# Attention's output projection as seven block products, and the gates' input sums made on VectorE during the attention

## The chip, the cores and the metric

One core of a Trainium2 chip runs the whole kernel as one program. The metric is the device time of one execution in microseconds, the median over several executions. TensorE (PE in the profile) does the matmuls, VectorE (DVE) and ScalarE (ACT) the elementwise work, GpSimd (POOL) a few elementwise operations and the issue of some DMAs, SyncE (SP) issues most other DMAs. Each engine takes its instructions in the order in which the program lists them and stops at the first one whose inputs, or whose place to write to, are not ready.

## The reference

A residual block on a sequence of 1024 tokens of width 1024, all in float32. Cut to what bears on the change:

```
xn = rmsnorm(x, norm1_g)
u  = xn @ w_in      # q,k,v of attention; f,i,q,g of the recurrence; gate_sb, gate_hg
o_sb = stick_breaking_attention(q_sb, k_sb, v_sb)        # 1024 x 512
o_hg = rmsnorm(hgrn2(...), hg_norm_g) * silu(g_hg)       # 1024 x 512
g_a  = sigmoid(gate_sb + b_gate[:1024])
g_b  = sigmoid(gate_hg + b_gate[1024:])
merged = g_a * (o_sb @ w_o_sb) + g_b * (o_hg @ w_o_hg)   # w_o_sb: 512 x 1024
h = x + merged @ w_out
h = h + square(relu(rmsnorm(h) @ w_ff1)) @ w_ff2
out = rmsnorm(h, final_g)
```

## The kernel before

Activations lie transposed: channels on the 128 partitions, tokens along the free dimension, in tiles of 128x1024 (two blocks of 128 channels by one half of 512 tokens, or one block by all 1024 tokens). A float32 product is made of three matmuls on operands that are split in a high part and a remainder: `three` issues high x high, high x remainder, remainder x high into one PSUM bank of 512 columns. The high part is a cast on ScalarE (`hi_copy`, rows CAST at L156), the remainder a subtraction on VectorE (`lo_sub`, rows TENSOR_TENSOR at L161). In names, a trailing `h` or `hi` is a high part, `l` or `lo` a remainder, `r` a raw tile as loaded.

The order in the program: norm and the first projections; then stick-breaking attention, in which each of the items (a head's block of queries) has scores `z`, a scan on VectorE (`rm`), a transpose on TensorE (`pw`), a split into `wTh` (ACT) and `wTl` (DVE), and the product `po`; between its pieces projection matmuls are interleaved by `st.advance`. Then the four heads of the HGRN2 recurrence, whose "main" pieces (`sl`, a score product that needs the ScalarE copy `ksl` of the keys made by `scores_of`; `pk`, `pkv`, `pho`, `pot`) alternate on TensorE with "fill" blocks. Fill blocks are `raw_job` (gate products that are kept in DRAM, `pga`, `pgq`), and then `sb_job`: attention's output projection, `pys`. After head 3 come the gates (`gates()`), with products `gX`, `gY` for ten gate blocks, and after that the merge, `w_out` and the MLP.

The parts that the change touches:

- **Attention's output projection.** `sb_job(cp)`, four units `wo00` to `wo03` of 256 output columns each. A unit's weights are one 128x1024 tile, split once (ACT and DVE). For each of its two blocks of 128 output channels and each half of the tokens, 4 channel blocks x 3 matmuls fill one bank `pys{cb}_{i}`: 4 x 2 x 2 x 12 = 192 matmuls. The first half is multiplied by the gate `g1r` (a DRAM load) on VectorE and stored by POOL, the second is copied by ScalarE (`ys`) and stored by ACT's queue. The attention output `osr` is split into `asbh`, `asbl` ahead of the projection. Three units lie among the recurrence's head 3; the last, `wo03`, lies in the gates: four steps after `y5` of the first gate block (`SB_HELD`), and the rest between `x7` and `y3`.
- **Inputs of the gates.** The gates are themselves block products with fewer multiplications (a Strassen-like scheme), so they need sums of quarters of the normed input `xn`. `whole_input` adds high part and remainder together by DMAs that accumulate (`xnl<-xnh`, eight of 512 KB on POOL's queue); then `sum_forms`, advanced a step at a time by the projection's loop, makes `gs` tiles by eight VectorE additions of 128x1024 and splits each (`gsh` on ACT, `gsl` on DVE).
- **Weight sums of `w_out`** are made by POOL's accumulating DMAs during attention, one per second item (`wsums`).

Instruction order on each engine is set by a scheduler from the order of this code and the declared dependencies (`after` adds one for order alone); tiles come from pools, and a tile's first writer waits for the last reader of the tile that had its place before. `slot` is a pool of 128x1024 tiles, `half` of 128x512, `wpool` has two tiles each of `raw`, `whi`, `wlo` kinds.

Of the kernel before, what the change touches and what calls it, by code (L numbers as in the profile page):

```python
# [2 lines left out]

# [6 lines left out]
F32 = mybir.dt.float32  # L10
F32R = mybir.dt.float32r
# [28 lines left out]
def kernel(  # L40
# [1264 lines left out]
            s = slice(half * 512, (half + 1) * 512)  # L1305
            return h[:, s], l[:, s]

    a_sb, a_hg = Split("asb"), Split("ahg")
    mgs = Acts("ms")
    def half(name, dt=F32):  # L1310
        return hpool.tile([P, 512], dt, tag="h", name=name)
# [87 lines left out]
    def raw_job(cb):  # L1399
        u = raw_units[cb]  # L1400

        def steps_of(ps, wt, w0, half_, k0, start):
            wh, wl = u.hl[wt]
            for k in range(4):
                c = (w0 + k) * P
                xh, xl = xn.mov(k0 + k, half_)
                three(
                    ps, wh[:, c : c + P], wl[:, c : c + P], xh, xl, start and k == 0, k == 3, True
                )
                if k % 2 == 1:  # L1410
                    yield

        def body():
            p1, p14, g1 = (half(f"{n}_{cb}") for n in ("p1", "p14", "g1"))
            ps, p4 = bank(f"pga{cb}"), bank(f"pgq{cb}")
            if 6 <= cb < KT:
                load_g1(cb - 6)
            if 5 <= cb < KT:
                sb_units[cb - 5].load()
            if 3 <= cb < KT - 1:  # L1420
                osb[cb - 3] = slot(f"osr{cb}")
                load(osb[cb - 3], od[cb - 3])
            yield from steps_of(ps, 0, 0, 0, 0, True)
# [7 lines left out]
            if cb == 3 or cb == KT - 1:  # L1431
                whole_input(1, int(cb == KT - 1))
# [8 lines left out]
            if 4 <= cb < KT:  # L1441
                a_sb.put(cb - 4, osb.pop(cb - 4))

        return st.add([u], body)

# [2 lines left out]
    def load_g1(cb):  # L1448
        g1r[cb] = half(f"g1r{cb}")
        load(g1r[cb], gd[cb])  # L1450

    forms, whole = {}, {}
    WAIT = 7

    def whole_input(i, j):
        for kp in range(2):
            h, l = (t.bitcast(F32) for t in xn.t[i, 2 * j + kp])
            nc.gpsimd.dma_start(l, h, accum_op=ALU.add)
            whole[i, j, kp] = l

    def sum_forms():


        raw = whole
        def split(m, kp, src):
            forms[m, kp] = tuple(slot(f"gs{n}{m}{kp}", F32R) for n in "hl")
            hi_lo(*forms[m, kp], src)

        for j in range(2):
            whole_input(0, j)  # L1470
        yield from range(WAIT)
        s1, s2 = {}, {}
        for kp in range(2):
            s1[kp] = slot(f"gs1{kp}")
            ins = add(s1[kp], raw[1, 0, kp], raw[1, 1, kp])
            if kp == 0:
                after(ins, hg_sum[0])
            yield
        for kp in range(2):
            split(5, kp, s1[kp])  # L1480
            yield
        for kp in range(2):
            s2[kp] = slot(f"gs2{kp}")
            sub(s2[kp], s1[kp], raw[0, 0, kp])
            yield
            split(6, kp, s2[kp])
            yield
        gates_in[0].load()
        gates_in[0].load_sums()
        for kp in range(2):  # L1490
            s3 = slot(f"gs3{kp}")
            sub(s3, raw[0, 0, kp], raw[1, 0, kp])
            split(7, kp, s3)
            yield
        gates_in[0].split()
        for kp in range(2):
            s4 = slot(f"gs4{kp}")
            sub(s4, raw[0, 1, kp], s2[kp])
            split(3, kp, s4)
            yield  # L1500
        gates_in[1].load()

    sb_units = []

    def sb_job(cp):
        src = W_OSB[:, cp * 256 : (cp + 1) * 256].rearrange("(k p) c -> p k c", p=P)
        unit = Unit(f"wo0{cp}", [[(0, 256, src)]])
        unit.roomy = (0,)
        sb_units.append(unit)

        def body():
            if cp == 0:
                side.append(sum_forms())
            for j in range(2):
                cb = 2 * cp + j
                if 1 < cb + 1 < KT:
                    load_g1(cb + 1)
                g1 = g1r[cb]
                for i, cs in halves():
                    ps = bank(f"pys{cb}_{i}")  # L1520
                    for _ in proj_half(
                        ps, unit.hl[0], a_sb.mov, 4, i, lambda k: k * 256 + j * P
                    ):
                        next(side[0], None)
                        yield
                    if i == 0:
                        mul(g1, ps, g1)
                        nc.gpsimd.dma_start(yd[cb][:, i, :], g1)
                    else:
                        y = half(f"ys{cb}")  # L1530
                        nc.scalar.copy(y, ps)
                        nc.scalar.dma_start(yd[cb][:, i, :], y)

        return st.add([unit], body)


    for h in range(1, NHS):
# [12 lines left out]
    f_job(3)  # L1550
    q_job(3)
    j_raw = [raw_job(cb) for cb in range(KT)]
    j_sb = [sb_job(cp) for cp in range(4)]

    class GatePair:
        def __init__(self, cb):
# [2 lines left out]
        def load(self):  # L1559
            cb = self.cb  # L1560
            self.raw = [
                wpool.tile([P, 1024], F32, tag="raw", name=f"wg{cb}r{i}") for i in range(2)
            ]
            for i, s_, which in ((0, 0, 0), (0, 1, 1), (1, 1, 1)):
                load(
# [72 lines left out]
        def gated(self, which, first, second):  # L1638
            h = 2 * (self.cb - KT) + which

            def rest(u2_sum):
                if which == 1:
                    muls(u2_sum)
                a_hg.put(h, ohg[h], u2_sum)

            def muls(behind=None):
                for (_, cs), t in zip(halves(), (first, second)):
                    after(mul(ohg[h][:, cs], ohg[h][:, cs], t), behind)

            if which == 0:  # L1650
                muls()
            owed_gated.append(rest)

        def x6(self):
# [741 lines left out]
    n_fill = 9 * (NHS - 1 + 5) + 10  # L2396
    n_first = 4
    ready = deque()
    wsums = out_weight_sums()
    done = 0  # L2400
    for i, it in enumerate(items):
        if i + 1 < len(items):
# [153 lines left out]
```

## Time and profile before

| | |
|---|---|
| median of 3 runs | 1419.76 us (1419.75 to 1419.99) |
| profiled execution, its own time | 1420.01 us |
| its span in the profile | 1418.2 us |
| granted TensorE clock, mean | 0.999 |
| TensorE, busy | 1408.0 us |
| VectorE, busy | 1049.5 us |
| ScalarE, busy | 659.3 us |
| GpSimd, busy | 145.0 us |

The span is what the trace covers; the time of the execution has 1.8 us more. Busy times are sums over instructions that overlap in part: a matmul's record is longer than the step to the next one, so TensorE's rate is read from start to start. Attention's products `po` lie between 91 and 327 us; the projection's matmuls `pys` between 511.7 and 573.6 us, with the first gate products `gX` from 554.7 us between them.

### The profile page before, as it was taken

What the parts mean: (1) busy time and instruction counts of PE and PEld (TensorE: products, weight loads), DVE (VectorE), ACT (ScalarE), POOL (GpSimd) and SP (SyncE); (2) the same over time, 40 slices, a digit from 0 to 9 for tenths busy, and PEclk for the clock granted to TensorE, in tenths of its full rate; (3) what the DMA queues carried; (4) which work ended last, traced back from release to release, by engine and by line L of the source; (5) the groups of instructions that cost most, each with busy time, mean ns of one, the idle gap of its engine ahead of it and who ended that gap; (6) DMA issues with size and microseconds to landing.
All of it is one profiled execution on the core that took longest, in us unless ns stands there. A gap on an engine that the chain in (4) does not pass through costs nothing.

```text
span 1418.2 us, 18602 instructions
## 1 busy us (share of the span) xinstructions
PE 1408.0 (99%) x6848; PEld 1183.5 (83%) x6848; DVE 1049.5 (74%) x1429; ACT 659.3 (46%) x1127; POOL 145.0 (10%) x282
## 2 busy tenths in 40 slices
PE   9999999999999999999999999999999999999998
PEld 7888888888888888888888888888888888888886
DVE  6667777778567888887788897676766657668765
ACT  6455555554243554433244764445444443534343
POOL 3011223110011031000000300000000000000042
PEclk9999999999999999999999999999999999999999
DMA  8344445435135685364585514444446974776725
GB/s 253 83 119 127 104 101 102 104 77 154 60 75 169 224 223 186 120 214 156 162 298 194 186 53 170 163 163 142 138 145 239 351 269 148 278 274 242 273 97 186
DMA packets 169730, 241.91 MB, mean 171 GB/s; under 512 B 30844, under 2 KB 97960, under 8 KB 169640
## 3 DMA queue, kind: packets, MB, share of 16 engines
q1 hardware_dynamic: 151432, 192.48, 41.0%
q0 software_dynamic: 11616, 34.61, 9.9%
q10 hardware_dynamic: 6592, 13.63, 2.7%
q8 instruction: 54, 0.88, 0.3%
q14 instruction: 36, 0.29, 0.1%
HBM read 170.43 MB, written 68.16 MB: 168 GB/s over the span
## 4 chain that ended last, share of the span: by engine, by line
PE 97%; ACT 1%; DMA 1%; DVE 1%; issue 0%; POOL 0%; SPq 0%; POOLq 0%; DVEq 0%; ACTq 0%
PE pm L128 21%; PE pX L128 9%; PE pW L128 6%; PE pY L128 6%; PE pjqk L128 6%; PE pga L128 4%; PE gX L128 4%; PE gY L128 4%; PE pjf L128 3%; PE pjq L128 3%; PE pys L128 3%; PE pji L128 3%; PE pyh L128 3%; PE po L128 3%; PE z L128 2%; PE pwX L128 2%
## 5 line engine op out<-in xcount | busy, mean ns | idle before, releaser
L854 DVE TENSOR_TENSOR_SCAN rm<-rm,bits 128x512 f32<-128x512 f32 (+6 forms) x72 | 87.5, 1222 | 30.5 <-ACT rm L835 29.0
L156 ACT CAST whid<-w 128x1024 fp32r<-128x1024 f32 x30 | 31.6, 1054 | 153.8 <-PE pm L128 85.4
L128 PE MATMUL pm<-wlod,sh 128*128 128x512 f32 x240 | 93.6, 390 | 0.0
L128 PE MATMUL pm<-whid,sl 128*128 128x512 f32 x240 | 93.5, 389 | 0.0
L128 PE MATMUL pm<-whid,sh 128*128 128x512 f32 x240 | 93.4, 389 | 0.0
L128 PE MATMUL pm<-tl,sh 128*128 128x512 f32 (+1 forms) x210 | 81.3, 387 | 0.0
L128 PE MATMUL pm<-th,sl 128*128 128x512 f32 (+1 forms) x210 | 81.3, 387 | 0.0
L128 PE MATMUL pm<-th,sh 128*128 128x512 f32 (+1 forms) x210 | 81.3, 387 | 0.0
L161 DVE TENSOR_TENSOR wlod<-w,whid 128x1024 fp32r<-128x1024 f32 x30 | 36.7, 1222 | 55.0 <-ACT whid L156 54.8
L156 ACT CAST wTh<-pw 128x512 fp32r<-128x512 f32 (+2 forms) x96 | 43.7, 482 | 62.4 <-PE pw L131 60.8
L161 DVE TENSOR_TENSOR wTl<-pw,wTh 128x512 fp32r<-128x512 f32 (+2 forms) x96 | 50.5, 548 | 28.9 <-ACT wTh L156 28.6
L161 DVE TENSOR_TENSOR sl<-sa,sh 128x1024 fp32r<-128x1024 f32 x56 | 68.2, 1218 | 0.6 <-ACT sh L156 0.6
L2173 POOL TENSOR_SCALAR fss<-fss 128x1 f32<-128x1 f32 x8 | 4.3, 543 | 562.0 <-ACT fsc L2168 561.5
L156 ACT CAST sh<-sa 128x1024 fp32r<-128x1024 f32 x56 | 57.2, 1045 | 7.8 <-DMA sa<-ad 7.8
L128 PEld LDWEIGHTS pm<-wlod,sh 128*128 128x128 f32 x240 | 45.1, 188 | 9.9 <-DVE wlod L161 0.4
L128 PEld LDWEIGHTS pm<-whid,sh 128*128 128x128 f32 x240 | 45.0, 188 | 9.4
L128 PEld LDWEIGHTS pm<-whid,sl 128*128 128x128 f32 x240 | 45.1, 188 | 9.2
L128 PE MATMUL pX<-sqh,t1l 128*128 128x512 f32 x128 | 50.0, 390 | 0.0
L128 PE MATMUL pX<-sql,t1h 128*128 128x512 f32 x128 | 50.0, 390 | 0.0
L128 PE MATMUL pX<-sqh,t1h 128*128 128x512 f32 x128 | 49.8, 389 | 0.0
L128 PEld LDWEIGHTS pm<-th,sh 128*128 128x128 f32 x210 | 39.5, 188 | 8.1
L128 PEld LDWEIGHTS pm<-tl,sh 128*128 128x128 f32 x210 | 39.4, 188 | 8.0
(936 smaller groups left out, 4358.8 us busy)
## 6 DMA issues: line engine op xcount, KB each, us to landing
w<-in_w_ff_dram SPq DMA_DIRECT2D x72, 512.0 KB, 4.8
sa<-ad SPq DMA_DIRECT2D x52, 512.0 KB, 6.8
ad<-a SPq DMA_DIRECT2D x32, 256.0 KB, 4.5
ad<-s SPq DMA_DIRECT2D x16, 512.0 KB, 3.2
tw<-in_w_out_dram POOLq DMA_DIRECT2D x24, 256.0 KB, 5.8
pr<-pd SPq DMA_DIRECT2D x10, 512.0 KB, 5.8
x<-in_x_dram SPq DMA_DIRECT2D x8, 512.0 KB, 7.9
xnl<-xnh POOLq DMA_DIRECT2D x8, 512.0 KB, 6.2
```

The lines of the kernel that those rows point to most:

```text
L128: return pe(nc.tensor.matmul(*a, **k))
L156: hi_last[0] = after(in_turn("act", nc.scalar.copy(dst, src)), hi_behind[0])
L161: nc.vector.tensor_tensor(out=dst, in0=src, in1=hi.bitcast(F32), op=ALU.subtract),
L854: sc = nc.vector.tensor_tensor_scan(out=rr, data0=rr, data1=bits[:, 1024 - nk + a : 1024 - nk + b][:, ::-1], initial=rm[:, b : b + 1] if i ...
L2173: nc.gpsimd.tensor_scalar(out=ssq, in0=ssq, scalar1=1.0 / D, scalar2=EPS, op0=ALU.mult, op1=ALU.add)
```

## The change

The projection `o_sb @ w_o_sb` becomes seven block products in place of eight. Weights and activations are taken as 2 x 2 blocks (256 input channels by 512 output channels; 256 input channels by 512 tokens). Seven products, in the order 2, 5, 3, 1, 6, 7, 4 (`SB_ORDER`), each of four banks (4 blocks of 128 output channels) x 2 channel blocks x 3 matmuls = 24 matmuls, 168 in all. Products 3, 6, 7 and 4 accumulate in PSUM on banks that stay open from an earlier product (`start` is true for 2, 5 and 1 alone), 5 and 3 share the names `pysY`, and 1, 6, 7, 4 share `pysX`. `end` takes each bank out: ScalarE copies after 2, 5, 3 and 4 (`aw`, `ay`, `az`), VectorE additions and subtractions after 1, 6 and 7, with the gate's multiplication where a sum is complete.

The weight blocks' sums (`tv1` to `tv4`) are made in DRAM by eight accumulating DMAs on POOL's queue during the attention, and are loaded as `wo{m}r`. Each of the seven weight blocks is split (`sb_split`: one CAST of 128x1024 on ACT, one subtraction on DVE), two products ahead. Activation blocks are summed on VectorE (`sb_sums`, eight operations of 128x512) and split (`sb_form`: `ash{m}`, `asl{m}`), one product ahead.

The gates' input sums are no longer made by `whole_input` and the eight additions: `input_sums` makes them from the high parts and remainders on VectorE, 18 operations of 128x1024 (`xs`, `xs4`), one per step of the attention's loop with `i > 2 and i % 5 > 1`, and POOL stores eight results to DRAM (`sx`). `sum_forms` then only loads them (`gs`) and splits them. The first gate block's raw weights move from `wpool` to `slot`; `SB_HELD` is 5 in place of 4 steps.

Cut to its core:

```diff
-    def whole_input(i, j):
-        for kp in range(2):
-            h, l = (t.bitcast(F32) for t in xn.t[i, 2 * j + kp])
-            nc.gpsimd.dma_start(l, h, accum_op=ALU.add)
+    def input_sums():
+        def step(out, a, b, op):
+            after(nc.vector.tensor_tensor(out=out, in0=a, in1=b, op=op), turn_lo[0])
+        for kp in range(2):
...
+            s = slot(f"xs{kp}")
+            step(s, h00, h10, ALU.subtract)
+            yield
+            step(s, s, l00, ALU.add)
...
+            step(s, s, l00, ALU.add)
+            stored(5, kp, s)
     def sum_forms():
...
-            ins = add(s1[kp], raw[1, 0, kp], raw[1, 1, kp])
+        for i, (m, kp) in enumerate(tiles):
+            fetch(i + 2)
+            yield
+            forms[m, kp] = tuple(slot(f"gs{n}{m}{kp}", F32R) for n in "hl")
+            hi_lo(*forms[m, kp], raw.pop(i))
+    def sb_split(m):
+        sb_w[m] = tuple(
+            wpool.tile([P, 1024], F32R, tag=t, name=f"wo{m}{t}") for t in ("whi", "wlo")
+        )
+        hi_lo(*sb_w[m], sb_raw.pop(m))
+    def sb_form(m):
+        h, l = sb_s[m] = tuple(slot(f"as{n}{m}", F32R) for n in "hl")
+        if m in (5, 6):
+            hi_lo(h, l, sb_sum[m])
+            return
...
+        def product(m, cp):
+            open_block("fill")
+            for k in range(2):
...
+                three(
+                    ps, wh[:, c : c + P], wl[:, c : c + P], sh[:, ks], sl[:, ks],
+                    start and k == 0, k == 1, True,
+                )
+        def end(m, cp, ps):
+            if m == 2:
+                sb_sum["w", cp] = half(f"aw{cp}")
+                nc.scalar.copy(sb_sum["w", cp], ps)
+                return
...
+            for m in ms:
+                n = SB_ORDER.index(m)
+                ahead = SB_ORDER[n + 1 : n + 3]
+                for cp in range(4):
+                    end(m, cp, product(m, cp))
+                    if cp == 0 and ahead:
+                        sb_split(ahead[0])
...
+                    if cp == 1 and ahead:
+                        sb_form(ahead[0])
+                    next(side[0], None)
-    j_sb = [sb_job(cp) for cp in range(4)]
+    j_sb = [sb_job(ms) for ms in ((2, 5), (3, 1), (6, 7), (4,))]
-    SB_HELD = {KT: 4}
+    SB_HELD = {KT: 5}
-        if i % 2 == 1:
+        if i % 2 == 1 or i % 8 == 0:
             next(wsums, None)
+        if i > 2 and i % 5 > 1:
+            next(insums, None)
```

Instructions move as follows at three places.

ScalarE, in the recurrence's head 3, at the score products of levels 4 and 5 (`ksl3_4` and `ksl3_5` are the key copies that the matmuls `sl3_4` and `sl3_5` wait for). Before:

```order
L1436 ACTIVATE g1_7_5035<-pga7_5036,prm_93 128x512
L1283 ACTIVATE on2_4806<-pot2_0_5125,prm_93 128x512
L1440 DMA gd7_128<-g1_7_5035 128x512
L1092 COPY ksl3_4_5152<-k3_4147 128x2x16x16
L1531 COPY ys0_5179<-pys0_1_5166 128x512
L1092 COPY ksl3_5_5212<-k3_4147 128x2x8x32
```

In the changed kernel, first around `ksl3_4`, then around `ksl3_5`:

```order
L1613 COPY aw0_5177<-pysW0_5170 128x512
L157 CAST ash5_5198<-as5_5075 128x1024
L1613 COPY aw1_5196<-pysW1_5189 128x512
L1093 COPY ksl3_4_5204<-k3_4196 128x2x16x16
L157 CAST gsh60_5225<-gs60_5185 128x1024
```

```order
L157 CAST ash3_5274<-osr5_4868 128x512
L157 CAST ash3_5274<-osr6_4963 128x512
L1619 COPY ay2_5289<-pysY2_5282 128x512
L157 CAST gsh50_5291<-gs50_5202 128x1024
L1093 COPY ksl3_5_5304<-k3_4196 128x2x8x32
```

The copies of the keys stood behind work that needs no matmul of the projection but `ys0`, one level later; now `ksl3_4` stands behind copies of the banks `pysW0` and `pysW1`, and `ksl3_5` behind a copy of `pysY2` and a cast of 128x1024.

ScalarE, at the end of head 3, where the projection's products 1, 6 and 7 lie in the changed kernel (`hon3_0` and `hon3_1` are squares of the head's output, `ash6`, `ash7` the high parts of activation blocks, `wo4whi` that of a weight block). Before:

```order
L156 CAST gsh61_5360<-gs21_5333 128x1024
L156 CAST gsh70_5381<-gs30_5379 128x1024
L156 CAST wo03h0_5406<-wo03r0_5241 128x1024
L1531 COPY ys3_5385<-pys3_1_5353 128x512
L1532 DMA yd3_134<-ys3_5385 128x512
L1272 ACTIVATE hon3_0_5390,hss3_0_5389<-pho3_0_5388 128x128 x4
L156 CAST gsh71_5421<-gs31_5419 128x1024
L156 CAST whig8_5433<-wg8r1_5371 128x1024
```

In the changed kernel:

```order
L157 CAST ash6_5460<-as6_5076 128x1024
L157 CAST gsh30_5492<-gs30_5375 128x1024
L157 CAST wo7whi_5535<-wo7r_5442 128x1024
L1273 ACTIVATE hon3_0_5510,hss3_0_5509<-pho3_0_5508 128x128 x4
L157 CAST gsh31_5541<-gs31_5410 128x1024
L1273 ACTIVATE hon3_1_5571,hss3_1_5570<-pho3_1_5569 128x128 x4
L157 CAST wo4whi_5605<-wo4r_5539 128x1024
L157 CAST ash7_5554<-osr3_4671 128x512
L157 CAST ash7_5554<-osr4_4765 128x512
```

Splits of activations and of weights now stand between the recurrence's rows: `ash6` ahead of product 6, and `ash7`, which product 7 needs, behind `wo4whi`, a weight block of product 4.

VectorE, in the attention (head 2's rows; `wTl2_2_0` is a remainder that the matmul `po` waits for). Before, and then in the changed kernel:

```order
L161 TENSOR_TENSOR QL4_1700<-pjqk4_1_1708,QH4_1699 64x512
L161 TENSOR_TENSOR wTl2_1_0_1806<-pw2_2_0_1809,wTh2_1_0_1805 128x3x128
L161 TENSOR_TENSOR wqk5l0_1826<-wqk5r0_1631,wqk5h0_1825 128x1024
L161 TENSOR_TENSOR wTl2_2_0_1764<-pw2_4_0_1841,wTh2_2_0_1763 128x4x128
L161 TENSOR_TENSOR wTl2_2_4_1766<-pw2_4_1_1848,wTh2_2_4_1765 128x128
```

```order
L162 TENSOR_TENSOR QL4_1731<-pjqk4_1_1739,QH4_1730 64x512
L162 TENSOR_TENSOR wTl2_1_0_1837<-pw2_2_0_1840,wTh2_1_0_1836 128x3x128
L1457 TENSOR_TENSOR xs1_1722<-xs1_1722,xnl01_257 128x1024
L162 TENSOR_TENSOR wqk5l0_1858<-wqk5r0_1658,wqk5h0_1857 128x1024
L162 TENSOR_TENSOR wTl2_2_0_1795<-pw2_4_0_1873,wTh2_2_0_1794 128x4x128
L162 TENSOR_TENSOR wTl2_2_4_1797<-pw2_4_1_1880,wTh2_2_4_1796 128x128
```

One of the 18 operations of `input_sums` stands between two of the attention's remainders.

More of the change, by code (lines that the diff above doesn't have):

```diff
@@ L2 @@
 from contextlib import ExitStack
+from itertools import chain
 import concourse.bass as bass
@@ L1422, in body @@
                 load(osb[cb - 3], od[cb - 3])
+            if cb == KT - 1:
+                sb_load(SB_ORDER[0])
+                side.append(sb_sums())
             yield from steps_of(ps, 0, 0, 0, 0, True)
@@ L1503 @@
[L1503 to L1509, printed above, removed]
-        def body():
[L1512 to L1534, printed above, removed]
+    forms = {}
@@ new lines, in sum_forms, with fetch @@
+    def sum_forms():
+        tiles = [(m, kp) for m in (6, 5, 7, 3) for kp in range(2)]
+        raw = {}
+        def fetch(i):
+            if i < len(tiles):
+                m, kp = tiles[i]
+                raw[i] = slot(f"gs{m}{kp}")
+                load(raw[i], sx[m][kp])
+        fetch(0)
+        fetch(1)
+        yield
+        for i, (m, kp) in enumerate(tiles):
+            fetch(i + 2)
+            yield
+            forms[m, kp] = tuple(slot(f"gs{n}{m}{kp}", F32R) for n in "hl")
+            hi_lo(*forms[m, kp], raw.pop(i))
+            if i == 2:
+                gates_in[0].load()
+                gates_in[0].load_sums()
+            if i == 4:
+                gates_in[0].split()
+            yield
@@ L1561, in load @@
             self.raw = [
-                wpool.tile([P, 1024], F32, tag="raw", name=f"wg{cb}r{i}") for i in range(2)
+                slot(f"wg{cb}r{i}")
+                if self is gates_in[0]
+                else wpool.tile([P, 1024], F32, tag="raw", name=f"wg{cb}r{i}")
+                for i in range(2)
             ]
@@ L2398 @@
     ready = deque()
-    wsums = out_weight_sums()
+    wsums = chain(out_weight_sums(), sb_weight_sums())
+    insums = input_sums()
     done = 0
```

175 lines of the change are left out of this document (130 added, 45 removed).

## The prediction

> **What bounds the kernel now.** I read the page first: busy shares and the chain that ended last.
>
> ```profile
> span 1418.2 us, 18602 instructions
> PE 1408.0 (99%) x6848; PEld 1183.5 (83%) x6848; DVE 1049.5 (74%) x1429; ACT 659.3 (46%) x1127; POOL 145.0 (10%) x282
> PE 97%; ACT 1%; DMA 1%; DVE 1%; issue 0%; POOL 0%; SPq 0%; POOLq 0%; DVEq 0%; ACTq 0%
> ```
>
> TensorE is the bound: 97% of the chain. Then TensorE's waits, whose columns are total, count and longest:
>
> ```profile
> PE warm L128 <- POOL ident masks.py:199: 2.3, 1, 2.3
> PE xnt L131 <- DVE x L653: 0.4, 1, 0.4
> ```
>
> The longest waits lie at the program's start, so every instruction reaches TensorE in time. A matmul fewer shortens the kernel by one step, and an input late by x lengthens it by x. The question is whether the changed order keeps all inputs in time. The stages, in windows (PE, weight loads, DVE, ACT, POOL; then granted clock, DMA share, GB/s):
>
> ```profile
> 140.00:180.00 40.00, 40.00 (x234) 34.76 (x233) 29.19 (x36) 23.46 (x53) 10.57 (x27) 1.00 0.49 107
> 512.00:540.00 28.00, 28.00 (x150) 23.60 (x150) 23.22 (x34) 14.49 (x25) 3.49 (x6) 1.00 0.92 259
> 540.00:560.00 20.00, 20.00 (x107) 17.01 (x106) 17.86 (x25) 11.36 (x28) 5.12 (x6) 1.00 0.46 159
> 574.00:600.00 26.00, 26.00 (x116) 21.53 (x116) 22.28 (x31) 11.47 (x16) 0.00 (x0) 1.00 0.41 133
> ```
>
> VectorE is busy 73% in attention, 83% and 89% in the projection, 86% in the first gates. The margin is in order, not in sums.
>
> **What is saved.** 192 matmuls become 168. The step between matmuls, from 24 consecutive ones (first and last row):
>
> ```profile
> 560.24 0.39 PE L128 MATMUL pys<-asbh,wo03h 128*128 128x512 f32 x1
> 565.45 0.39 PE L128 MATMUL pys<-asbh,wo03l 128*128 128x512 f32 x1
> ```
>
> (565.45 - 560.24) / 23 = 0.2265 us, so 24 x 0.2265 = 5.44 us less. The record of 0.39 is longer than the step, so a bank's last record ends 0.39 - 0.23 = 0.16 after the next matmul's slot. [...]
>
> **Score products of head 3.** ScalarE before, with TensorE's rows between:
>
> ```profile
> 513.46 0.62 ACT L1092 COPY ksl<-k 128x512 f32<-128x512 f32 x1
> 514.37 0.39 PE L128 MATMUL pys<-asbh,wo00l 128*128 128x512 f32 x1
> 514.60 1.05 PE L128 MATMUL sl<-q,ksl 128*128 128x128 f32 x8
> 518.00 0.39 PE L128 MATMUL pys<-asbh,wo00l 128*128 128x512 f32 x1
> 518.42 0.59 ACT L1531 COPY ys<-pys 128x512 f32<-128x512 f32 x1 [4.35 <-PE pys L128]
> 518.90 0.62 ACT L1092 COPY ksl<-k 128x512 f32<-128x512 f32 x1
> 519.42 1.05 ACT L156 CAST gsh<-gs 128x1024 fp32r<-128x1024 f32 x1
> 520.37 0.69 ACT L1283 ACTIVATE on<-pot,prm 128x512 f32<-128x512 f32 x1
> 522.77 1.05 PE L128 MATMUL sl<-q,ksl 128*128 128x128 f32 x8
> ```
>
> They give the prices: hand-over from TensorE 0.03 (518.00 + 0.39 to 518.42); a bank's copy holds ScalarE for 0.48 (518.42 to 518.90), a 128x1024 cast for 0.95 (519.42 to 520.37); a `ksl` copy takes 0.62. Both `ksl` ended long before their `sl`: 514.08 against 514.60, 519.52 against 522.77.
>
> Level 4 now: `ksl3_4` stands behind `aw1`, a copy of `pysW1`, whose last matmul is the one directly ahead of `sl3_4`. It stands where the row of 514.37 stands and ends at 514.76; `aw1` starts at 514.79, `ksl3_4` at 515.27 and ends at 515.89, `sl3_4` starts at 515.92 in place of 514.60: 1.3 us of stall.
>
> Level 5: `sl3_5` follows directly on bank `pysY2`, and ScalarE has `ay2`, `gsh50`, `ksl3_5`. From the slot of `sl3_5`: 0.16 + 0.03, then 0.48 + 0.95 + 0.62 and 0.03 = 2.3 us. Queued behind are only ScalarE's next splits. Bounds of the two: nothing less than 3.6 in all, since the order alone sets them; at most 1 us more if ScalarE is late by one cast.
>
> **Products 6 and 7.** VectorE's prices:
>
> ```profile
> 508.23 1.21 DVE L161 TENSOR_TENSOR wo00l<-wo00r,wo00h 128x1024 fp32r<-128x1024 f32 x1
> 509.36 0.68 DVE L169 TENSOR_TENSOR k<-k,pp 128x512 f32<-128x512 f32 x1
> 509.97 0.68 DVE L1314 TENSOR_TENSOR p<-p,pgq 128x512 f32<-128x512 f32 x1
> 539.54 0.60 PE L128 MATMUL pho<-v,sc 128*128 128x128 f32 x4
> 539.99 0.39 PE L128 MATMUL pho<-k,q 128*128 128x128 f32 x2
> 551.12 0.60 PE L131 MATMUL pot<-ident,hon 128*128 128x128 f32 x4
> 551.47 0.48 PE L128 MATMUL pys<-asbh,wo02h 128*128 128x512 f32 x1
> ```
>
> A 128x1024 operation takes 1.21 and holds VectorE for 1.13, a 128x512 one 0.68 and 0.61. Four `pho` matmuls take 0.45, four `pot` 0.35.
>
> Product 6: the tile of `ash6` is free only after product 1's last matmul, which reads the tile's former holder. From that matmul's end slot: 0.16 + 0.03, cast 1.05, hand-over 0.03, `asl6` 1.22, 0.03 = 2.5. TensorE has four `pho` and one matmul meanwhile (0.45 + 0.23): 1.8 us of stall. Bounds: 0, if the tile comes free earlier than its wait reads (a rival below), to 3.0, with `gsl71` (1.13) in front of `asl6` just begun.
>
> Product 7: `wo4whi` stands ahead of `ash7` on ScalarE and waits for the last matmul but one of product 6 (two weight tiles). From the end slot of product 6: it starts at -0.03, `ash7`'s first half at 0.92 and ends at 1.51 (as a 128x512 copy, 0.59); `asl7`'s first half starts at 1.54, `ay1`'s multiplication follows at 2.15, the second half at 2.76, ending at 3.44; its matmul at 3.47. Without waits TensorE would be there after four `pot` and four matmuls, 0.35 + 0.91 = 1.26: 2.2 us. Bounds: 0, if a weight tile is free early, to 3.2, with one cast of 0.95 more ahead on ScalarE. I take the walked values, since each step has its row.
>
> **VectorE's load.** Removed in this stage: four activation remainders and four weight remainders, eight sums, eight multiplications; added: seven weight remainders, the sums and remainders of blocks, gate arithmetic. Net about 10 us by these prices, while the windows show 28.00 - 23.22 + 20.00 - 17.86 = 6.9 us idle; the stalls give 7.6 us back, so it is covered, without margin. The 24 saved matmuls go between the first gate block's `x7` and `y3`, which takes cover from the splits of the next gate:
>
> ```profile
> 590.65 0.68 DVE L1314 TENSOR_TENSOR gu<-pr,gX 128x512 f32<-128x512 f32 x1
> 595.79 1.29 DVE L1314 TENSOR_TENSOR pr<-pr,gX 128x512 f32<-128x512 f32 x2 [0.39 <-PE gX L128]
> ```
>
> VectorE waited 0.39 for TensorE there and 3.7 in the whole window: 5.44 less TensorE work could show at most 5.44 - 3.72 = 1.7. I take 0.3, near the end where the stalls ahead have let VectorE catch up; ends 0 and 1.7.
>
> **Input sums in attention.** 18 operations x 1.13 = 20.3 us of VectorE among the rows of heads 0 to 4 of eight, so in about the first 130 us of attention. At the place of the third order listing:
>
> ```profile
> 162.34 0.69 DVE L161 TENSOR_TENSOR KS<-pjqk,KS 64x512 fp32r<-64x512 f32 x1 [1.46 <-ACT QH L156]
> 165.25 0.87 DVE L161 TENSOR_TENSOR wTl<-pw,wTh 128x512 fp32r<-128x512 f32 x2
> 166.84 0.28 PE L128 MATMUL po<-wTl,V 128*128 128x256 f32 x1
> 181.98 0.19 PEld L128 LDWEIGHTS po<-wTl,V 128*128 128x128 f32 x1 [0.22 <-DVE wTl L161]
> ```
>
> The remainder that `po` needs at 166.84 ended at 165.25 + 0.68 = 165.93: 0.91 of margin against 1.13 pushed in, 0.2 of stall. The tightest place, 181.98, has its `xs` row behind the remainder. Others fall into idle time like the 1.46 above. I take 0.2; ends 0 and 2 (two places by 1.13). The eight stores to DRAM, their loads, and the weight sums replace DMAs whose issue and landing no engine waited for:
>
> ```profile
> xnl<-xnh POOLq DMA_DIRECT2D x8, 512.0 KB, 6.2
> ```
>
> **Sum.** -5.44 + 1.3 + 2.3 + 1.8 + 2.2 + 0.3 + 0.2 = +2.7 us. The profiled execution took 1420.01 (its span and 1.8 around it), so 1422.7; its time is 0.25 above the median of the runs, which stays inside what I can tell.
>
> **Rivals.** 0.2% of 1419.76, 2.84 us, is about the least that a measurement of this kernel can tell from no change: same is 1416.9 to 1422.6.
>
> - *The whole saving arrives*: ScalarE and VectorE are early and the copies don't hold `ksl`. 1420.0 - 5.4 = 1414.6. Against it: a copy can't start before its bank is done. 0.10.
> - *Only the score products stall*: the tiles for `ash6`, `ash7` come free earlier than their waits read. -5.44 + 3.6 + 0.5: 1418.7. The waits could be met while TensorE does other blocks. 0.25.
> - *Attention overloads VectorE* (slower): 29.19 of 40 becomes 35.4 with 20.3 us over 130. It decides when a second `xs` comes before the backlog of the first is gone; then four or five tight places, like those of 0.91 and 0 margin above, lose about 1.1 each: 1422.7 + 4.5 = 1427. Against it: idle times of 1 to 1.5 us between remainders. 0.12.
> - *The clock falls* (slower): at the program's end TensorE idles after 1411.77.
>
> ```profile
> 1411.49 0.28 PE L128 MATMUL pm<-th,sl 128*128 128x256 f32 x1
> 1412.00:1415.00 3.00, 0.00 (x0) 0.00 (x0) 1.83 (x6) 2.26 (x6) 1.09 (x2) 1.00 0.69 255
> 1415.00:1418.20 3.20, 0.00 (x0) 0.00 (x0) 0.00 (x0) 0.00 (x0) 0.00 (x0) 0.54 0.50 166
> ```
>
> The clock stayed at 1.00 for 3.2 us of idleness and was 0.54 after. If the stall of product 7 passes 3.2 us, it costs 1.0 more itself and, if the clock then stays low for about as long, 3.2 x 0.46 = 1.5: 1425.2. 0.06. [...]
>
> **Numbers.** My forecast has 0.45, spread about evenly round its limit of 1422.6; 0.02 is left for a transfer landing late. Faster: 0.10 and a little of the second case, 0.13. Same: the rest of the second and near half of the forecast, 0.42. Slower: 0.45. The range, with the bounds: low, score stalls without the others, and a little less, 1416.9; high, +2.7 with product 7, gates and attention at or near their upper ends (1.0 + 1.4 + 1.8), 1426. The forecast's own range is 1420.5 to 1425.
>
> **What would show it.** In the changed profile: 168 `pys` matmuls; TensorE waits for ScalarE before `sl` near 1.3 and 2.3, and for `asl6` and `asl7` near 1.8 and 2.2; the first gate's `gX` begins near 562.5 in place of 554.7; VectorE busy about 30 us more; clock 0.999. I am wrong if those waits are missing (then the saving arrives), or if waits of `po` for `wTl` add over 2 us.

## The result

| | before | changed |
|---|---|---|
| median of 4 runs, us | 1419.88 | 1433.69 (1432.47 to 1434.24) |
| ratio to before, 95% interval | | 1.0096 [1.0078, 1.0113] |
| profiled execution, us | 1420.01 | 1434.24 |
| its span, us | 1418.2 | 1432.1 |
| granted clock, mean | 0.999 | 0.995 |

The change made the kernel 13.8 us slower. The forecast was 1422.7 with a range up to 1426.0; slower was the likeliest direction, but the time lies 7.7 above the range. The profile's page of the changed kernel, in the lines that answer to those of before:

```profile
span 1432.1 us, 18657 instructions
PE 1411.1 (99%) x6824; PEld 1183.2 (83%) x6824; DVE 1078.6 (75%) x1470; ACT 669.9 (47%) x1146; POOL 153.1 (11%) x294
PE 93%; DVE 2%; ACT 2%; DMA 1%; issue 1%; POOL 0%; SPq 0%; POOLq 0%; ACTq 0%; DVEq 0%
```

TensorE issues 24 matmuls fewer and is busy 3.1 us longer: its matmuls have become slower somewhere. Its share of the chain fell from 97% to 93%, so there are waits too. TensorE's waits (total, count, longest):

```profile
PE sl L129 <- ACT ksl L1093: 3.8, 2, 2.5
PE gY L129 <- DVE pr L1315: 2.6, 1, 2.6
PE pysX L129 <- DVE asl L162: 2.5, 2, 1.7
PE pysX L129 <- ACT ash L157: 1.7, 2, 1.5
```

The rows in which they lie, from TensorE's timeline (start, length of the record; the bracket has the idle time ahead):

```profile
516.96 1.16 PE L129 MATMUL sl<-q,ksl 128*128 128x128 f32 x8 [1.29 <-ACT ksl L1093]
527.92 1.16 PE L129 MATMUL sl<-q,ksl 128*128 128x128 f32 x8 [2.49 <-ACT ksl L1093]
...
529.73 0.63 PE L129 MATMUL pysY<-ash,wo5wlo 128*128 128x512 f32 x1
530.15 0.63 PE L129 MATMUL pysY<-ash,wo5whi 128*128 128x512 f32 x1
...
548.65 0.50 PE L129 MATMUL pysX<-asl,wo6whi 128*128 128x512 f32 x1 [0.76 <-DVE asl L162]
558.58 0.50 PE L129 MATMUL pysX<-ash,wo7whi 128*128 128x512 f32 x1 [1.50 <-ACT ash L157]
560.78 0.80 PE L129 MATMUL pysX<-asl,wo7whi 128*128 128x512 f32 x1 [1.70 <-DVE asl L162]
...
596.47 0.50 PE L129 MATMUL gY<-gsh,whig 128*128 128x512 f32 x1 [2.57 <-DVE pr L1315]
```

The two rows without a bracket are the surprise: 530.15 - 529.73 = 0.42 from start to start in place of 0.2265, and records of 0.63 in place of 0.39. TensorE ran at about half speed there. Windows of 3.41 us show it (PE busy, granted clock, DMA share, GB/s):

```profile
515.30:518.71 3.41, 2.12 (x14) 1.00 1.03 408
525.54:528.95 3.41, 1.03 (x9) 1.00 0.93 351
528.95:532.36 3.41, 3.41 (x11) 0.50 0.06 22
556.27:559.68 3.41, 1.31 (x7) 1.00 0.31 110
559.68:563.09 3.41, 2.31 (x6) 0.50 0.74 245
563.09:566.51 3.42, 3.42 (x10) 0.50 0.35 134
593.82:597.23 3.41, 0.84 (x4) 1.00 0.70 201
597.23:600.64 3.41, 3.41 (x9) 0.50 0.92 292
```

Behind each of three windows in which TensorE was busy for only 0.84 to 1.31 of 3.41 us stands a stretch at a granted clock of 0.50, once a double one. The low stretches start at 528.95, 559.68 and 597.23. That is 30.73 and 37.55 us from each other, 9 and 11 times 3.414, and one low stretch lasts 3.41: their starts lie on a grid, 1.03, 1.10 and 0.76 us behind the end of a wait (527.92, 558.58, 596.47). From start to start, the matmuls in the three places lose 1.6, 2.4 and 1.6 us against the usual step, 5.6 us in all.

The sum, from the start of one matmul to the next, against the usual step:

| term | forecast | measured |
|---|---|---|
| 24 matmuls less | -5.44 | -5.4 |
| attention, input sums | 0.2 | 0.9 |
| level 4 | 1.3 | 1.45 |
| level 5 | 2.3 | 2.65 |
| product 6 | 1.8 | 1.4 |
| product 7 | 2.2 | 4.0 |
| gates | 0.3 | 2.7 |
| clock | 0 | 5.6 |
| sum | +2.7 | +13.3 |

TensorE's last matmul starts 13.5 us later than before (1425.02 against 1411.49); the spans differ by 1432.1 - 1418.2 = 13.9, so 0.4 lies behind it. TensorE's part arises between attention and the second gate block. The gate products of the changed kernel start and end as follows (in the kernel before: 554.7 to 703.7):

```profile
L129 PE MATMUL gX<-gsh,whig x40: 389/389/474, 569.1 to 717.2; 128*128 128x512 f32 x40
```

+14.4 at the first, +13.5 at the last; from there on the lag stays within 0.1.

### The profile page after: what moved, and what is told of

Its sections match the earlier page's. It is cut to its first block, busy times and chain, and to the rows that moved or that the text cites. A ratio compares the mean times of both kernels' runs of the same rounds, so it can differ in the third digit from the quotient of the medians.

```text
span 1432.1 us, 18657 instructions
## 1 busy us (share of the span) xinstructions
PE 1411.1 (99%) x6824; PEld 1183.2 (83%) x6824; DVE 1078.6 (75%) x1470; ACT 669.9 (47%) x1146; POOL 153.1 (11%) x294
## 4 chain that ended last, share of the span: by engine, by line
PE 93%; DVE 2%; ACT 2%; DMA 1%; issue 1%; POOL 0%; SPq 0%; POOLq 0%; ACTq 0%; DVEq 0%
PE pm L129 21%; PE pX L129 9%; PE pW L129 6%; PE pY L129 6%; PE pjqk L129 6%; PE gY L129 4%; PE pga L129 4%; PE gX L129 3%; PE pjf L129 3%; PE pji L129 3%; PE pyh L129 3%; PE po L129 3%; PE pjq L129 2%; PE z L129 2%; PE pwX L129 2%; PE pjv L129 2%
## 5 line engine op out<-in xcount | busy, mean ns | idle before, releaser
L129 PEld LDWEIGHTS pm<-th,sl 128*128 128x128 f32 x210 | 39.4, 188 | 8.1
```

What stands on the lines that cost most here:

```text
L129: return pe(nc.tensor.matmul(*a, **k))
```

## The experiments

The expectations were written before the runs; "the run with four edits" in them is e7, "with the forms alone" e2. Times are medians, beside 1419.97 to 1420.06 for the kernel before.

**What idleness costs (e4).** The kernel before, with idle time put ahead of matmuls of the MLP:

```diff
+    def hold(t, n):
+        at = t[:, 0, 0:1]
+        for _ in range(n):
+            nc.gpsimd.tensor_scalar(out=at, in0=at.bitcast(F32), scalar1=1.0, scalar2=0.0, op0=ALU.mult, op1=ALU.add)
...
+                        if tb == 2 and o is ops[i][0] and 1 < i < NST - 4:
+                            hold(o[3], 1 + (i - 2) % 8)
```

> The kernel before, with 24 places of idleness of chosen length put in its last third (MLP down projections): one to eight dependent GpSimd operations (times 1.0) on a column of a weight tile that the next matmuls read, three ladders of eight. Each step should add about 0.5 us of TensorE idleness. It measures what the idleness itself costs. Theory A (the clock is granted by stretches of a free-running grid of 3.41 us, and a stretch with only about a third of busy time is followed by one at half clock): the shortest steps, 1 to 3 operations, cost their length alone; the longest, 7 or 8 operations (3.5 us and more), always or nearly always cost a stretch at about 0.5, which is 1.7 us more; steps of 2 to 3 us cost it sometimes, by where they fall in the grid, and the low stretches begin at whole multiples of 3.41 us from each other. Rival (a fixed length of uninterrupted idleness decides, wherever it falls): one threshold parts the steps, every step above it is followed by a low stretch and none below it.

One execution took 1486.6 us. Its 22 waits, 0.2 to 6.7 us long, came to 47.7 us; 66.5 us were added. A wait makes the step from start to start about 0.3 us longer than itself (2.35 for one of 2.06, 1.32 for one of 1.02), 7 us in all; the rest, 12 us, fits the half clock, at which TensorE was busy for 24 us. First the waits, then windows on the grid of this run (PE, weight loads, DVE, ACT, POOL; clock, DMA):

```profile
PE pm L128 <- POOL whid L2300: 47.7, 22, 6.7
...
1215.72:1219.13 3.41, 0.87 (x4) 0.74 (x5) 1.07 (x1) 0.00 (x0) 2.01 (x6) 1.00 1.05 398
1219.13:1222.54 3.41, 3.41 (x10) 2.63 (x9) 0.00 (x0) 0.00 (x0) 0.00 (x0) 0.50 0.39 157
1266.92:1270.33 3.41, 1.63 (x8) 1.01 (x6) 2.28 (x2) 0.00 (x0) 2.21 (x3) 1.00 1.06 414
1270.33:1273.75 3.42, 2.10 (x9) 1.76 (x10) 1.22 (x2) 0.00 (x0) 1.19 (x2) 1.00 0.23 92
1283.98:1287.40 3.42, 1.13 (x5) 0.96 (x6) 1.91 (x2) 0.00 (x0) 2.07 (x3) 1.00 1.04 401
1287.40:1290.81 3.41, 3.41 (x10) 2.64 (x9) 0.00 (x0) 0.00 (x0) 0.00 (x0) 0.50 1.05 399
1328.36:1331.77 3.41, 1.51 (x7) 0.94 (x5) 2.61 (x3) 0.00 (x0) 2.16 (x5) 1.00 0.18 32
...
1423.93:1427.34 3.41, 2.66 (x6) 2.16 (x7) 0.37 (x1) 0.00 (x0) 2.44 (x7) 0.50 0.84 289
1427.34:1430.76 3.42, 3.42 (x9) 2.65 (x8) 0.00 (x0) 0.50 (x1) 1.74 (x5) 0.50 0.88 324
1430.76:1434.17 3.41, 2.52 (x11) 1.69 (x9) 2.83 (x3) 2.46 (x3) 1.42 (x2) 1.00 0.01 6
```

The five waits of 3.44 us and more were followed by half clock, the seventeen of up to 3.10 were not, so theory A's "sometimes" for 2 to 3 us came out as never here. The wait of 3.10 lies across two windows, which keep 1.63 and 2.10 of work, and nothing follows; that of 3.44 leaves one window with 1.13, and half clock follows. The five drops begin at 1219.1, 1287.4, 1314.7, 1420.5 and 1437.6, which is 20, 8, 31 and 5 times 3.413 apart ((1437.6 - 1219.1) / 64 = 3.414): these lie on one grid, too. Once low, a window of 2.66 busy did not end it, a full one did (the last three rows; the same in the changed kernel, 2.31 and 3.42). Other runs lie between: 2.84 ended it in e9, 2.82 and 3.12 did not in e5 and e12.

By itself the ladder also fits the rival, a fixed length between 3.10 and 3.44. The changed kernel's runs exclude that: half clock came after single waits of 2.49 and 2.57, and the wait of 2.57 before `gY` was followed by it in two profiles (the changed kernel, e1) and not in two others (e2, e5), where the same wait lay otherwise in the grid. In e2 it ran from 591.33 to 593.90; the grid of that run, from a drop at 527.64, has a border at 592.50, and no window lost more than 1.4 us. In these traces it is thus the work in a window of the grid that parts the cases, and not the length of a wait. The border is not settled further than this: over all traces of this case, from 20 us after the start on, each of the 17 windows of the grid with at most 1.31 us of matmul records was followed by half clock; of the 33 with 1.51 to 2.12 us four were (1.63 in e6, 1.69 in e11, 1.71 in e10, 2.12 in e1, against 2.12 without it at 515.30 in the changed kernel); none with more was. A matmul's record is longer than its step (0.39 us against 0.2265), and windows of 2.12 stand on both sides, so busy time as the profile counts it does not part them all.

**The input sums alone (e3).** The kernel before with `input_sums` and the loading `sum_forms`; the output projection as before.

```diff
-    def whole_input(i, j):
...
-            nc.gpsimd.dma_start(l, h, accum_op=ALU.add)
...
+    def input_sums():
...
+        if i > 2 and i % 5 > 1:
+            next(insums, None)
```

> The kernel before with only the gates' input sums changed: 18 operations on VectorE in the attention, stored and loaded again, the projection as it was in four units. Theory A: TensorE loses what the changed kernel lost before the projection began, 0.9 us (the projection begins at 512.65 against 511.74), and the eight additions saved beside the projection bring nothing, since nothing waited for them: 1420.8, same. Rival C (VectorE's load in attention is the larger part of the loss, and the late waits follow from it): 1425 or more.

1422.39 us, ratio 1.0018 [1.0009, 1.0027]: the sums cost 2.4 us alone. By the start of the first `pys` the lag is 0.6 us, of which attention has 0.4 and `sd` 0.2; the rest is one wait:

```profile
526.06 1.16 PE L128 MATMUL sl<-q,ksl 128*128 128x128 f32 x8 [1.43 <-ACT ksl L1092]
```

The cast `wo02h`, which starts only at 524.44, now stands ahead of `ksl3_5` on ScalarE; theory A, which had 1420.8, had missed that. Attention itself lost 0.4: rival C is out.

**Gate block 9 first (e6).** The changed kernel with `pr` and its sums ahead of gate block 0's splits:

```diff
-            if n and v.cb:
+            if n and v.cb not in (0, KT + 1):
                 next_pair(n, m, v.u2_sum if v.cb < KT else None)
...
-            if not v.cb:
+            if v.cb in (0, KT + 1):
                 next_pair(n, m, v.y_sum)
```

> The changed kernel with gate block 9's additions (pr and ahgl of the ninth gate block's third product) ahead of the first attention weights' splits on VectorE, not behind them. Theory A: the wait gY<-pr of 2.6 us at 596 us goes, and with it the stretch at half clock behind it (1.6 us): 1433.7 - 2.6 - 1.6 = 1429.5 us, range 1428.5 to 1431.5. Rival B (VectorE is merely late there, and the next reader waits in its place, since wg9's raw tile came 15 us later than before): 1432 or more, with the wait at another tile of gates 0 or 9.

1428.07 us, ratio 1.0061 [1.0048, 1.0073]: 5.6 us better than the changed kernel by the medians. The five times fall in two groups, 1427.7 to 1428.1 and 1430.0 to 1430.2, and the profiled execution, 1430.04, is of the upper one: 4.2 better than the changed kernel's profile. The wait before `gY` is gone, and with it the low stretch at 597, 2.6 + 1.6, which is these 4.2. Behind product 7 one low stretch stands in place of two, but this kernel came to it later and waited longer for `ash` (2.32), so that at the first `gX` the two profiles are level within 0.1. What the faster group saves besides, no trace shows; it puts the median just below theory A's range. Theory A holds in its mechanism: it was the place of `pr` behind five splits, and the clock added more than half of the wait again. From the first `gX` to the end the lag falls by 5.1, the saving, now that no wait hides it.

**Ends one step later (e1), forms two ahead (e2), both (e5).** Each attacks the waits in the projection.

```diff
 # e1
-                    end(m, cp, product(m, cp))
+                    ps = product(m, cp)
+                    yield
+                    end(m, cp, ps)
...
-                    yield
 # e2
-                    if cp == 1 and ahead:
+                    if cp == 1 and n == 0:
                         sb_form(ahead[0])
+                    if cp == (2 if n == 0 else 1) and len(ahead) > 1:
+                        sb_form(ahead[1])
```

> The changed kernel, but what follows a block of a product (copying its bank out, splitting the next blocks, the gates' forms) is written one step later, so that the key copies ksl3_4 and ksl3_5 stand ahead of aw1, ay2 and gsh50 on ScalarE. Theory A (each wait of TensorE is set by the order on ScalarE and VectorE at its own place, and an idle time of some 2.5 us also costs a stretch of half clock): the waits of sl for ksl (3.8 us by the waits view) go, and so does the half clock from 529.0 to 532.3 (about 1.65): 1433.7 - 5.5 = 1428.2. Rival B (ScalarE and VectorE have too much work in this stage, so time gained at one place is lost at the next): the waits at products 6 and 7 grow by as much, and the time stays within 1 us of 1433.7.

1433.76 us, 1.0100 [1.0086, 1.0113]: nothing gained, as rival B had it. The waits for `ksl` went, as theory A said, and others came in their place: 1.13 at product 1, and longer ones behind it:

```profile
557.54 0.66 PE L132 MATMUL pot<-ident,hon 128*128 128x128 f32 x4 [1.87 <-DVE hon L170]
562.82 0.80 PE L129 MATMUL pysX<-asl,wo7whi 128*128 128x512 f32 x1 [3.47 <-DVE asl L162]
```

> The changed kernel, but the activation blocks of a product are split two products ahead in place of one (ash6, ash7 and their remainders stand ahead of product 1's and 6's end). Theory A: the waits of pysX for ash and asl (4.2 us by the waits view, some 5 with the matmuls lost between them) go, and the half clock of 559.8 to 566.75 (two stretches, about 3.0) with them: 1433.7 - 7.5 = 1426.2, with the two waits for ksl still there. Rival B: the tiles held longer make the gates' forms late, and the time lost appears at the first gX: over 1431.

1431.17 us, 1.0079 [1.0066, 1.0092]: 2.5 better, and rival B's figure. TensorE no longer waits for `ash` and `asl`; 1.9 for `ay` and 1.2 for `hon` came instead, in the projection and not, as rival B said, at the first `gX`.

> Both edits: what follows a block one step later, and the activation blocks two products ahead. Theory A: all four waits and two of three half-clock times go: 1433.7 - 13 = 1420.7 if the wait of gY for pr in the gates (2.6 us, and 1.6 of half clock after it) stays as it is, and 1416.5 if it was a consequence of product 7's lateness and goes as well. Rival B: over 1428.

1431.77 us, 1.0080 [1.0067, 1.0093], where theory A had at most 1420.7. `sl` waits 0.7 in place of 3.8, no form waits, but `pot` waits 3.18 for `hon`, and two low stretches follow. Theory A was too simple: taking a wait away at its place doesn't bring its length. Why `hon` is late was the next question.

**The half tiles (e12, e7).** `hon3_0` takes the place of a half tile that `aw1` had, and so waits for `aw1`'s store to DRAM. e12 is e5 with e6's gates; e7 is e12 with

```diff
-    N_FULL, N_HALF = 40, 10
+    N_FULL, N_HALF = 39, 12
```

> The run with ends one step later and forms two ahead (1431.8), with gate block 9's additions ahead of gate 0's splits, and the room as it was (40 full, 10 half tiles). It parts the half tiles from the gates' order in the run with four edits (1425.4). Theory A (the half tile that hon3_0 shares with aw1 made the 3.2 us at pot, and the stretch at half clock behind it): this run keeps both, 1431.8 - 2.6 - 0 to 1.7 = 1427.5 to 1429.2, so that the half tiles are worth 2 to 4 us. Rival B (the half tiles do nothing): 1425 to 1426.3.

> The changed kernel with four edits: each product's end written one step later (ksl ahead of it), forms made two products ahead, gate block 9's additions ahead of the first gate block's splits, and two full tiles' room turned into two more half tiles (39 full and 12 half in place of 40 and 10). Theory A (what e5 had left is the half tile that hon3_0 shares with aw1, 3.2 us at pot, and gY<-pr 2.6 us, each with up to one stretch at half clock, 1.7 us): both waits go, and 1431.8 comes down by 3.2 + 2.6 and one or two stretches, to between 1422 and 1426 us; where the whole of the saved matmul time of 5.4 us then shows, 1417. Rival B (the work on VectorE and ScalarE in this stretch is too much, so that the wait moves on to another tile): over 1428, with a wait of 2 us or more at pot, pysX or X.

e12: 1428.48 us, 1.0059 [1.0047, 1.0072]. e7: 1425.42 us, 1.0038 [1.0025, 1.005]. Two half tiles more, at the price of one full tile, are worth 3.1 us; the full tile given up shows as a wait of 0.5 us of `pX` for `t1l` at 861 us, which e7 and e8 have and e12 has not. In e12, ScalarE's row of `hon` and what TensorE waits for it:

```profile
554.38 0.28 ACT L1273 ACTIVATE hon<-pho 128x128 f32<-128x128 f32 x1 [2.79 <-DMA yd<-aw]
...
557.70 0.89 PE L132 MATMUL pot<-ident,hon 128*128 128x128 f32 x4 [4.03 <-DVE hon L170]
```

In e7 `hon` starts at 548.17 with no wait, no wait of TensorE in this stage is longer than 1.14, and the clock is 1.00 throughout it:

```profile
551.81 0.50 PE L129 MATMUL pysX<-ash,wo6whi 128*128 128x512 f32 x1 [0.53 <-DVE aw L1315]
557.77 0.50 PE L129 MATMUL pysX<-ash,wo7whi 128*128 128x512 f32 x1 [1.14 <-DVE ay L1318]
560.27 0.63 PE L132 MATMUL pot<-ident,hon 128*128 128x128 f32 x4 [0.84 <-DVE hon L170]
```

Both expectations of theory A held. It is still 5.4 us slower than before.

**The same with the ends as in the change (e8).**

> As the run with four edits, but with each product's end where the changed kernel has it (ksl behind it). Theory A: sl<-ksl keeps its 3.8 us and one stretch at half clock (1.7 us); gY<-pr (2.6 us) goes, and pysX<-ay and pot<-hon (1.9 and 1.2) go as far as the half tiles caused them: 1431.2 - 2.6 - 1.2 = 1427.4, range 1425 to 1429.5. Rival B (the half tiles are not what hon and ay wait for): about 1428.6 or more, with pot<-hon and pysX<-ay as in the run with the forms alone.

1428.77 us, 1.0060 [1.0047, 1.0074], where both theories have a part of their ranges: `pot` waits no longer (1.2 less), but `ay` waits 2.7 in place of 1.9, and the two waits for `ksl` keep their 3.8 and one low stretch. Against e2 it is 2.4 better, about the wait before `gY` alone, so the half tiles seem to have brought nothing here (no run has them without the gates' order). Beside e7 it shows what the later ends are worth once half tiles are there: 3.4 us. Without them, from e2 to e5, they brought nothing. By these runs the two help only together.

**What is left in e7 (e10, e9, e11).** VectorE in e7 (PE, weight loads, DVE, ACT, POOL):

```profile
536.00:548.00 12.00, 11.15 (x65) 9.35 (x63) 11.59 (x18) 7.97 (x11) 1.08 (x2) 1.00 0.46 143
548.00:560.00 12.00, 8.79 (x40) 5.99 (x39) 11.39 (x19) 7.02 (x23) 6.04 (x8) 1.00 0.76 275
```

11.59 and 11.39 of 12 us: nothing is left there. e10 leaves the eight multiplications out, e9 puts them on GpSimd, and e11 moves a form besides:

```diff
 # e9                                    (e10: the line goes)
         def gated(cb, t):
-            mul(t, t, g1r.pop(cb))
+            nc.gpsimd.tensor_tensor(out=t, in0=t, in1=g1r.pop(cb), op=ALU.mult)
 # e11, besides
+                    if m == 7 and cp == 3:
+                        sb_form(4)
```

> The run with four edits without the eight multiplications by the gate: the projection's output isn't gated, the rest is computed. It takes 4.9 us of work off VectorE in this stage and puts nothing elsewhere. Theory A (VectorE's load is what is left): waits between 536 and 562 us, 4.1 us and their restarts, fall by 2.5 to 5: 1420.5 to 1423. Rival B (the order and latencies of single chains are what is left, not the load): 1424.5 or more, with the same waits in the same places.

1423.16 us, 1.0022 [1.0013, 1.0031]. 4.9 us less work on VectorE brought 2.3, just short of theory A's 2.5: the waits for `aw` and `ay` are gone, those behind ScalarE (`ksl` 0.67, `pp` 0.84) stay, and `hon` with `wo7wlo` (1.22 and 0.48) fell into one window and cost a low stretch. VectorE's load is a good part of what is left, not all.

> The run with four edits, and the eight multiplications of the projection's sums by the gate (128x512) on GpSimd in place of VectorE. In the run with four edits VectorE was busy 11.6 of 12 us (536 to 548) and 11.4 of 12 (548 to 560), and the waits left there (pp, aw, hon, wo7wlo, ay, hon: 4.1 us) all come last by it or by work queued behind it. Theory A (what is left is VectorE's load in this stage): 8 x 0.61 = 4.9 us of it go, waits fall by 2 to 4 us: 1425.4 comes down to 1421.5 to 1423.5. Rival B (GpSimd's multiplications, about 2 us each by its 0.96 us for 128x256, stand in front of hn_y, for which hon waits): 1425 or more, with pot<-hon at 2 us or more.

1429.91 us, 1.0066 [1.0052, 1.0080]: rival B, and more than it said. Rows of GpSimd and VectorE:

```profile
540.17 1.65 POOL L1607 TENSOR_TENSOR aw<-aw,g1r 128x512 f32<-128x512 f32 x1
544.99 2.20 POOL L1607 TENSOR_TENSOR aw<-aw,g1r 128x512 f32<-128x512 f32 x1 [2.29 <-DVE aw L1315]
...
540.58 2.33 DVE L162 TENSOR_TENSOR wo6wlo<-wo6r,wo6whi 128x1024 fp32r<-128x1024 f32 x1
542.83 1.21 DVE L162 TENSOR_TENSOR wlog<-wg8r,whig 128x1024 fp32r<-128x1024 f32 x1
545.95 2.32 DVE L162 TENSOR_TENSOR gsl<-gs,gsh 128x1024 fp32r<-128x1024 f32 x1
...
552.42 1.28 POOL L1607 TENSOR_TENSOR aw<-aw,g1r 128x512 f32<-128x512 f32 x1 [4.36 <-DVE aw L1315]
...
552.50 0.68 DVE L1318 TENSOR_TENSOR ay<-ay,pysX 128x512 f32<-128x512 f32 x1
553.10 1.69 DVE L162 TENSOR_TENSOR gsl<-gs,gsh 128x1024 fp32r<-128x1024 f32 x1
```

A 128x1024 subtraction that VectorE began while GpSimd multiplied took 1.69 to 2.33 in place of 1.21, five times for the eight multiplications. Each ended 1.08 or 1.09 us behind GpSimd's end (540.17 + 1.65 = 541.82 and 540.58 + 2.33 = 542.91), as if it had waited for it; operations with an input in PSUM, as the one at 552.50, kept their 0.68. Together VectorE lost 4.1 of the 4.9 us taken off it. New waits for `k` (1.8 us in three places) came with it, and `pot` waits 2.6 for `hon`.

> As the run with the multiplications on GpSimd, and the activation form of product 4 (a cast and two remainders, 1.2 us on VectorE) made after product 7 and not in product 6, so that the stage before the gates has 1.2 us less work on VectorE and ScalarE. Theory A: 1 us less than that run, 1420.5 to 1422.5; a kernel no slower than before (1420.0) only if nearly all waits go. Rival B: the same as that run within 0.7 us, since waits there come by GpSimd or by transfers.

1429.19 us, 1.0063 [1.0051, 1.0076]: 0.7 below e9, between the two theories' differences, and far above theory A's 1422.5; up to product 7 the waits are the same. No run was faster than the kernel before; of those with seven products and the whole output, e7 is the best.

## Why the prediction was wrong

Two steps failed. The sum had the clock at nothing, and it cost 5.6 us. And VectorE's load was held to be "covered, without margin", while its late work made product 7 cost 4.0 in place of 2.2 and the gates 2.7 in place of 0.3. Term by term:

- **The saving** was right: 5.1 us show from the first `gX` on in e6, where nothing hides them.
- **Level 4 and level 5** were right, 1.45 and 2.65 against 1.3 and 2.3, and **product 6** nearly, 1.4 against 1.8. Orders that follow from the program alone can be walked by prices of rows.
- **Product 7** was mis-sized: 4.0 against 2.2, past its bound of 3.2. The walk let VectorE take `asl7` as soon as its high part was there. It stood behind `wo7wlo`, two operations on `ay` and a `gsl`, which themselves were late: `hon` had stopped VectorE for 1.68, for `hn_y`, which is made from ScalarE's `hon`, and that had waited 0.94 for the store of `aw`, as in e12. A second error hid a part of the first: the walk let the matmul wait for both halves of `asl7`, but it started at 560.78, behind the first (560.04 + 0.68 = 560.72). The sentence that failed is the one on VectorE's load, "covered, without margin".
- **Gates** failed by most of a term: 2.7 against 0.3, bound 1.7. The estimate set VectorE's wait in the window of before against the saved matmuls. But the sums `pr` of gate block 9 stand at the end of a queue of splits, and these began late, since the raw tile `wg0r` came late: SyncE's three issues of `wg9r` took 9.23 us, 7.8 of them a wait for VectorE's `wo4wlo`, and `wg0r` was issued at 576.74, against 561.59 before. In e6 it is issued as late, and TensorE does not wait: the order of `pr` behind the splits was needed too. SyncE's rows, then VectorE's:

```profile
557.86 9.23 SPq L137 DMA_DIRECT2D wg9r<-in_w_in_dram  x3
576.74 1.50 SPq L137 DMA_DIRECT2D wg0r<-in_w_in_dram  x3
...
581.04 0.69 DVE L1318 TENSOR_TENSOR wg0r<-wg0r 128x512 f32<-128x512 f32 x1 [2.59 <-DMA wg0r<-in_w_in_dram]
...
595.13 0.69 DVE L162 TENSOR_TENSOR wol<-wor,woh 128x512 fp32r<-128x512 f32 x1
595.73 0.68 DVE L1315 TENSOR_TENSOR pr<-pr,gY 128x512 f32<-128x512 f32 x1
```

- **The clock** is the largest miss, 5.6 us. The rival on it took 3.2 us of unbroken idleness as its condition, from the one row at the program's end, and 0.06 as its chance. In three places, with no single wait above 2.6 us, half clock followed, each time behind a window of the grid with 0.84 to 1.31 us of work. That stalls of up to 2.3 us cost their length alone was the author's estimate, which no row showed, and it did not hold: half clock began at 559.68 behind waits of 1.50 and 1.70, which lay mostly in one window.
- **Attention** cost 0.2 by its own end as forecast, and 0.7 at `sd` behind it. VectorE's busy time rose by 29.1 us, as forecast (30).

Without the clock, the sum would have been +7.7, or 1427.7, past the range's end: product 7 and the gates alone, 4.2 above their terms, lead to 1426.9, and the clock nearly doubles what is lost. All upper bounds of the prediction together would have given -5.4 + 4.6 + 3.0 + 3.2 + 1.7 + 2.0 = +9.1, or 1429.1, so even they do not reach the measured time without the clock. Of the rivals, the whole saving did not arrive, products 6 and 7 did stall, and attention was not overloaded.

## What to carry to other kernels

In these runs a stall of TensorE cost its length and 0.1 to 0.3 us more (2.65 for a wait of 2.49, 2.35 for one of 2.06), and besides it about 1.6 us for each low stretch full of matmuls (1.6 from 528.95 and from 597.23 on). Here 2.1 us and more of idleness within one 3.41-us window, in one wait or in several, was always followed by one, 1.3 to 1.9 us sometimes. Where the grid lay differed from profile to profile (a border at 593.82 in the changed kernel, at 592.50 in e2); that the changed kernel's runs spread by 1.8 us, and those of before by 0.6, fits this. Before crediting a saved matmul, walk the elementwise engines' queues through the stage at their busy share: where VectorE was busy 95% to 97%, as in e7, waits that were taken away came back at the next tile. Look for pools as well as orders: two small tiles were worth 3.1 us here, and an order that brought nothing without them brought 3.4 with them.

## What the runs showed of the hardware that was not expected

In these traces the stretches at a granted clock of 0.50 started on a grid of 3.41 us (9 and 11 times 3.414 apart in the changed kernel, 20, 8, 31 and 5 times 3.413 in e4). Behind a window of the grid with at most 1.31 us of matmul records one followed in 17 of 17 cases, with 1.51 to 2.12 us in 4 of 33, with more in none; a wait of 3.10 us that lay across two windows was followed by none (e4). A low stretch with 2.31 (the changed kernel) or 2.66 us (e4) of busy time was followed by another, one with 3.15 (e5 and e12) or 3.41 was not.

A 128x1024 subtraction on VectorE ended 1.08 or 1.09 us behind a GpSimd multiplication that it met, after up to 2.33 us in place of 1.21 (e9), and VectorE lost by this 4.1 of the 4.9 us taken off it, so GpSimd was no free place for work in this stage, where VectorE was busy 11.59 and 11.39 of 12 us (e7). The multiplications of 128x512 themselves took 1.26 to 2.20 us there against 0.68 on VectorE. All five slowed subtractions have both inputs in SBUF, and the operations with one input in PSUM kept their time (0.68 at 552.50). Why they differ, no run shows.
